# Modulation blocks moved from the first mixer to three later places in a two-block transformer kernel

## The chip, the cores and the metric

One core of a Trainium2 chip runs the whole program. The metric is the device time of one execution in microseconds (us). The kernel works in fp32: every product of two matrices is made of three matmuls (high x high, high x low, low x high) of operands that were split into a rounded part and a rest.

## The reference, cut to what matters

A first block has two layers (an even one with a Hyena and attention mixer, an odd one with a retention mixer, each with an MLP behind it); a second block follows and is not touched. Each layer's shifts, scales and gates come from a modulation: one product of two conditioning vectors with a 1024 x 6144 matrix.

```python
for i in range(DEPTH):
    mod_l = (c_act @ ada_w[i] + ada_b[i])[:, None, :]
    mod_c = cc_act @ ada_w[i] + ada_b[i]
    sh_a, sc_a, g_a, sh_m, sc_m, g_m = jnp.split(mod_l, N_MOD, axis=-1)
    ...
    h_l = modulate(rms_norm(x, norm_mix_g[i]), sh_a, sc_a)
    ...  # mixer: even or retention, gives y_l
    x = x + g_a * y_l
    x = x + g_m * sq_relu_mlp(modulate(rms_norm(x, norm_mlp_g[i]), sh_m, sc_m), mlp_w1[i], mlp_w2[i])
```

Of the second layer's modulation, the shift and scale `sh_a`, `sc_a` are wanted by the norm ahead of the retention, the gate `g_a` by the retention's out-projection, `sh_m`, `sc_m` by the norm ahead of the second MLP, and `g_m` by the end of that MLP.

## The kernel before, in words

Activations lie with features on the 128 partitions and 512 latent plus 256 context tokens along the free axis. The program (`program`, L307) goes in order through the first layer's mixer (`mixer0`), the first MLP, the retention (`retention`, four heads, two directions each), the second MLP, the second block and its expert stage.

**Modulation** (`ada`, L451). A layer's modulation has 12 blocks of 512 outputs: blocks 0 to 3 are `sh_a`, `sc_a`; 4 and 5 `g_a`; 6 to 9 `sh_m`, `sc_m`; 10 and 11 `g_m`. A block reads four chunks of 128 x 1024 fp32 (512 KB); for each chunk TensorE runs four narrow matmuls (L486; the profile counts two passes of each, so eight rows a chunk). Then ScalarE copies the sum out of PSUM (L459), two small matmuls turn it (L464, four passes), and VectorE adds the bias (L468); for blocks 3 and 9 it also makes `1 + scale` (L477).

**The weight stream** (`Stream`, L117). Every weight of the program goes through one stream, in the order in which TensorE asks for it (a first build of the program records that order). SP issues each load (L148) into one of five raw slots of 512 KB (four, and a fifth from the end of the first mixer on). A normal chunk is then split: ScalarE casts it (L155) and VectorE takes the difference (L157) into one of three pairs of split buffers, after which its raw slot is free. A modulation chunk is not split (`uncut`, L122): it keeps its raw slot until TensorE has used it (`done`, L201). So loads can run ahead of TensorE by five raw chunks and three split ones, and nothing is loaded out of order.

**The first mixer** (L703). Three generators share the stretch, drawn by a clock of given costs (`until`, L839): the in-projection with the Hyena behind it (`hy`), the attention (`attn0`), and `more` (L820), which runs the first layer's blocks 4 to 11 and then all 12 blocks of the second layer.

**Norms and tails.** A norm (`norm_mod`, L515) sums squares (L538, L541), adds over the partitions with a matmul of ones (L566), takes root and reciprocal (L502, L503), and scales, shifts and splits the eight tiles one after the other (L526, L527, L287, L288). Norms are traced as tails that run in between the next matmuls (`later`, `tick`, `settle`). The retention's last direction (L1109) ends with a norm of its own for each half of the tokens: squares (L1161, L1163), products (L1166), a matmul of ones (L1168), root and reciprocal, products (L1173), sums and splits (L1253, L287, L288); then its out-projection follows, half by half, and the second MLP, whose first group of four tiles also goes half by half (L972).

**Order on the engines.** The framework's planner runs a simulated timeline and fixes the order of the instructions on each engine, with the program's order as priority; each engine then executes its queue in that order and waits where something is late. Slots and buffers are given out by hand as the program is traced.

Of the kernel before, what the change touches and what calls it, by code (L numbers as in the profile page):

```python
# [208 lines left out]
def drain(*gens):  # L209

    gens = [list(g) if isinstance(g, tuple) else [g, 1.0] for g in gens]
    clock = [0.0] * len(gens)
    live = list(range(len(gens)))
    while live:
        i = min(live, key=lambda j: clock[j])
        try:
            clock[i] += next(gens[i][0]) / gens[i][1]
        except StopIteration:
            live.remove(i)


class K:
# [56 lines left out]
    def mm3(self, ps, wh, wl, xh, xl, start, stop):  # L279
        mm = self.nc.tensor.matmul  # L280
        mm(ps, wh, xh, start=start, stop=False)  # L281
        mm(ps, wh, xl, start=False, stop=False)  # L282
        mm(ps, wl, xh, start=False, stop=stop)  # L283

    def split(self, hi, lo, x):

# [20 lines left out]
    def program(self):  # L307
        nc = self.nc
        a = self.a
        self.ws = ws = Stream(self, self.order)  # L310
        self.phase(*MIX0)
        self.consts()
        for i in range(4):
            ws.add("cs", [a["cs_l"][i]])
        ws.add("cs", [a["cs_c"]])
        for nb in range(12):
            ws.add("ada0", [a["ada"][0, nb, i] for i in range(2)])
        order = [16, 17, 12, 13, 14, 15] + [x for c in range(4) for x in (8 + c, 4 + c)] + [0, 1, 2, 3]
        for n in range(9):
            ws.add("evin", [a["ev_in"][n]])  # L320
        self.ev_order = order
        for m in ("cs", "ics"):
            for q in "lc":
                src = a[f"{m}_{q}"]
                for i in range(4 if q == "l" else 1):
                    ws.add(m, [src[i] if q == "l" else src])
        for n in range(4):
            ws.add("evout", [a["ev_out"][n]])
            ws.add("evout_c", [a["ev_out"][n]])
        for nb in range(12):  # L330
            ws.add("ada1", [a["ada"][1, nb, i] for i in range(2)])
        G = 4
        self.G = G
        for l in range(2):
            for g in range(FF // 128 // G):
                ws.add("w1", [a["w1"][l, g * G // 2 + i] for i in range(G // 2)])
                ws.add("w2", [a["w2"][l, g, i] for i in range(G // 2)])
            ws.add("w1_b", [a["w1"][l, i] for i in range(G // 2)])
            ws.add("w2_b", [a["w2"][l, FF // 128 // G - 1, i] for i in range(G // 2)])
        for h in range(4):  # L340
            ws.add("od", [a["od_in"][h, i] for i in range(8)])
            ws.add("odo", [a["od_out"][h, i] for i in range(2)])
        ws.add("od_c", [a["od_in"][0, 1]])
        ws.add("odo_b", [a["od_out"][3, i] for i in range(2)])
        for n in range(7):
            ws.add("in2", [a["w_in2"][n]])
            ws.add("in2_b", [a["w_in2"][n]])
        for n in range(4):
            ws.add("out2", [a["w_out2"][n]])
            ws.add("out2_b", [a["w_out2"][n]])  # L350
        for n in range(8):
            ws.add("wq", [a["w_q"][n]])
            ws.add("wq_b", [a["w_q"][n]])
        ws.add("u", [a["ud"][n] for n in range(64)])
        ws.add("v", [a["vd"][n] for n in range(64)])
        ws.pump()

        self.ada_prep()
        self.maskr, self.identr = self.R(384), self.R(128)
        self.hb = [self.RP(T) for _ in range(KT)]  # L360
        self.h = [(b.hi.ap, b.lo.ap) for b in self.hb]

        def first():
            yield from self.ada(0, range(4))
            for seg in (LAT, CTX):
                for k in range(KT):
                    self.stat(k, seg)
                yield from self.norm_mod(0, 0, seg, self.h)

        self.ws.rest = nc.vector  # L370
        filt = self.hy_filter()
        drain(self.until((first(), 1.5), (filt, 1.0)))
        self.mark("mix0")
        drain(self.mixer0(filt))
        self.phase(*MLP)
        self.mark("mlp0")
        drain(self.mlp(0, True, lambda seg: self.norm_mod(1, 0, seg, self.h)))
        self.phase(*RET)
        self.mark("ret")
        drain(self.retention())  # L380
        self.phase(*MLP)
        self.mark("mlp1")
        drain(self.mlp(1, False, self.norm_final))

        for b in self.mod + self.sc1:
            b.free()
        self.phase(*B2)
        self.mark("blk2")
        drain(self.block2())
        self.phase(*PEER)  # L390
        self.mark("peer")
        drain(self.peer())
# [310 lines left out]
    def mixer0(self, filt):  # L703
        nc = self.nc
# [3 lines left out]
        qkv = self.F(6 * T)  # L708
# [4 lines left out]
        vt = self.F(6 * 128)  # L713
# [85 lines left out]
        hyx0 = self.F(4 * T)  # L799
        hyz = self.F(4 * T)  # L800
# [18 lines left out]

        def more():  # L820
            yield from self.ada(0, range(4, 12))
            yield from self.ada(1)

        yield from self.both((hy(), 1.0), (self.attn0(range(6), yah, yal), 1.2), (more(), 0.7))
        self.ws.rest = nc.vector
        self.ws.free.append(self.F(1024, top=True))
        for b in (qkv, vt, hyx0, hyz, self.maskr, self.identr, self.c32, self.kinds):
            b.free()
        yt = [t for b in (yy[0], ya) for t in self.tiles(b, T)]
        self.load_x()  # L830
# [90 lines left out]
    def mlp(self, l, ctx, then):  # L921

        nc = self.nc
# [7 lines left out]
        parts = [LAT, CTX] if ctx else HALF  # L931
# [38 lines left out]
        def w1(g):  # L970
            a = acts[g % 2]
            if g == 0:  # L972

                banks = []
                for key, (c0, c1) in zip(("w1", "w1_b"), parts):
                    for i in range(G):
                        w = self.ws.get(key)
                        ps = self.bank() if ctx or c0 == 0 else banks[i]
                        o = 0 if ctx else c0
                        gemm(w, h, 0, ps.ap[:, o : o + c1 - c0], (c0, c1))  # L980
                        self.ws.done()
                        if ctx:
                            later(up, a, i, [(ps, (c0, c1))])
                        elif c0 == 0:
                            banks.append(ps)
                        else:
                            later(up, a, i, [(ps, LAT)])
                        self.tick()
                        yield 0.01 * (c1 - c0)
                    self.settle()  # L990
                self.ws.rest = nc.vector
                return
            for i in range(G):
                w = self.ws.get("w1")
                res = [(self.bank(), seg) for seg in segs]
                for ps, seg in res:
                    gemm(w, h, 0, ps.ap[:, : seg[1] - seg[0]], seg)
                self.ws.done()
                later(up, a, i, res)
                yield 0.01 * W  # L1000
# [42 lines left out]
    def retention(self):  # L1043
        nc = self.nc
# [61 lines left out]
                a.free()  # L1106
                b.free()

        def direction(d, qk, v, tab, g, after, done, parts, add):  # L1109

            q, k = qk
            qh, ql = q.hi.v(2, S), q.lo.v(2, S)
# [22 lines left out]
            for n, (t, i0, m, m0) in enumerate(js):  # L1135
                ps = self.bank()
# [19 lines left out]
            for c0, c1 in parts:  # L1156
                m = c1 - c0
                acc = self.F(m)
                for c in range(4):
                    sq = self.F(m)  # L1160
                    nc.scalar.activation(sq.ap if c else acc.ap, o[c].ap[:, c0:c1], AF.Square)  # L1161
                    if c:
                        nc.vector.tensor_add(acc.ap, acc.ap, sq.ap)  # L1163
                    sq.free()
                for c in range(4):
                    nc.vector.tensor_mul(g[:, c, c0:c1], o[c].ap[:, c0:c1], g[:, c, c0:c1])  # L1166
                ps = self.bank()
                nc.tensor.matmul(ps.ap[:, :m], self.ones.ap, acc.ap, start=True, stop=True)  # L1168
                acc.free()
                r = self.rstd(ps.ap[:, :m], 512, m, self.eps6.ap[:, 0:1])  # L1170
                ps.free()
                for c in range(4):
                    nc.vector.tensor_mul(g[:, c, c0:c1], g[:, c, c0:c1], r.ap)  # L1173
                    if add:
                        add(c, c0, c1)
                r.free()
# [4 lines left out]
        for hd in range(4):  # L1181
# [27 lines left out]
            v = self.RP(6 * 512)  # L1209
# [15 lines left out]
            for d in range(2):  # L1225
                g = self.F(4 * S)
# [24 lines left out]
                def add(c, c0, c1):  # L1251
# [2 lines left out]
                    self.split(y.hi.v(4, S)[:, c, c0:c1], y.lo.v(4, S)[:, c, c0:c1], a)  # L1254

                yield from direction(d, (q, k), v, tabs[d], gv, after, done, HALF if d == 1 and hd == 3 else [LAT],
                                     add if d else None)
            for g in gs:
                g.free()
            prev = y  # L1260
# [1276 lines left out]
```

## Time and profile before

| | |
|---|---|
| median of 3 runs | 3834.04 us (3833.3 to 3835.98) |
| profiled execution | 3846.21 us |
| its span, first to last instruction | 3844.5 us |
| TensorE matmuls busy | 3598.5 us, 94% of the span |
| TensorE weight loads busy | 3168.7 us, 82% |
| VectorE busy | 2461.9 us, 64% |
| ScalarE busy | 1455.4 us, 38% |
| GpSimd busy | 711.4 us, 19% |
| mean granted clock of TensorE | 0.971 |

The profiled execution is a single one and slower than the runs without a profile; all durations below are its own. Busy shares are averages over stages with different limits, so the stages are read one by one. In the profile PE is TensorE's matmuls, PEld its weight loads, DVE VectorE, ACT ScalarE, POOL GpSimd, SP the engine that issues the stream's loads. A value in brackets behind a row is the idle time of the engine just ahead of it and what ended it.

### The profile page before, as it was taken

The numbers are of one execution on the slowest core, as the hardware profiler recorded it, in microseconds if no ns is written. First come the engines' busy times: TensorE is split into PE (matmuls) and PEld (weight loads), VectorE is DVE, ScalarE is ACT, GpSimd is POOL, SyncE is SP. The second block draws the span as 40 slices with busy tenths as digits, with TensorE's granted clock in tenths as the row PEclk, the third lists the DMA queues.
The fourth block names the chain that finished last, engine by engine and source line by source line (L and its number), as shares of the span: only waits on it lengthen the run. The fifth ranks groups of instructions, "written<-read, shape, count | busy, mean of one in ns | idle before, by whom it ended". The sixth has DMA issues, their size and how long they took to land. (4 is left out here: it accounts for less than half of the span.)

```text
span 3844.5 us, 51080 instructions
## 1 busy us (share of the span) xinstructions
PE 3598.5 (94%) x20063; PEld 3168.7 (82%) x20063; DVE 2461.9 (64%) x4157; ACT 1455.4 (38%) x2351; POOL 711.4 (19%) x511
## 2 busy tenths in 40 slices
PE   7999899999999999998999898888889999999997
PEld 4766588888888888887888867878789999889997
DVE  6543675343466555657544657898988777777754
ACT  5323444222244333335323546425633333332332
POOL 1111100000000000000000110665534444444200
PEclk9999999999999999998999998999999999999998
DMA  5355432212122212122322312324788888888732
GB/s 204 118 197 187 151 127 85 65 62 65 62 95 89 73 63 86 58 75 72 115 95 97 129 60 95 102 85 143 211 309 313 305 304 308 291 302 298 269 126 72
DMA packets 199597, 573.38 MB, mean 149 GB/s; under 512 B 17051, under 2 KB 67227, under 8 KB 199356
## 3 DMA queue, kind: packets, MB, share of 16 engines
q1 hardware_dynamic: 100224, 362.33, 28.7%
q0 software_dynamic: 42416, 156.57, 11.4%
q10 hardware_dynamic: 56716, 51.22, 4.0%
q8 instruction: 157, 2.57, 0.3%
q14 instruction: 84, 0.69, 0.0%
HBM read 539.64 MB, written 30.41 MB: 148 GB/s over the span
## 5 line engine op out<-in xcount | busy, mean ns | idle before, releaser
L155 ACT CAST ra<-fa 128x1024 fp32r<-128x1024 f32 x591 | 620.1, 1051 | 1591.6 <-PE P L282 655.0
L157 DVE TENSOR_TENSOR ra<-fa,ra 128x1024 fp32r<-128x1024 f32 x543 | 663.0, 1223 | 491.2 <-ACT ra L155 484.2
L282 PE MATMUL P<-ra 128*128 128x512 f32 (+1 forms) x1952 | 694.5, 357 | 2.9 <-DVE ra L288 2.7
L283 PE MATMUL P<-ra 128*128 128x512 f32 (+1 forms) x1872 | 675.3, 363 | 2.4 <-DVE ra L157 2.4
L281 PE MATMUL P<-ra 128*128 128x512 f32 (+1 forms) x1824 | 651.0, 364 | 21.1 <-ACT ra L287 17.4
L283 PE MATMUL bank<-ra 128*128 128x384 f32 (+2 forms) x1648 | 564.4, 343 | 63.1 <-DVE ra L157 41.8
L281 PE MATMUL bank<-ra 128*128 128x384 f32 (+2 forms) x1648 | 561.7, 342 | 13.0 <-ACT ra L287 11.4
L282 PE MATMUL bank<-ra 128*128 128x384 f32 (+2 forms) x1648 | 560.0, 340 | 8.3 <-DVE ra L288 8.3
L281 PE MATMUL P<-mR,ra 128*128 128x512 f32 (+1 forms) x1344 | 464.7, 349 | 12.8 <-ACT mR L287 8.6
L283 PE MATMUL P<-mR,ra 128*128 128x512 f32 (+1 forms) x1344 | 459.2, 343 | 0.3 <-DVE ra L157 0.3
L282 PE MATMUL P<-mR,ra 128*128 128x512 f32 (+1 forms) x1216 | 424.3, 350 | 1.0 <-DVE mR L288 1.0
L282 PEld LDWEIGHTS P<-ra 128*128 128x128 f32 x1952 | 375.4, 192 | 56.1 <-DVE ra L288 3.7
L281 PEld LDWEIGHTS P<-ra 128*128 128x128 f32 x1824 | 346.7, 192 | 78.7 <-ACT ra L287 19.5
L283 PEld LDWEIGHTS P<-ra 128*128 128x128 f32 x1872 | 357.9, 191 | 57.7 <-DVE ra L157 3.7
L283 PEld LDWEIGHTS bank<-ra 128*128 128x128 f32 x1648 | 317.7, 193 | 79.9 <-DVE ra L157 53.2
L281 PEld LDWEIGHTS bank<-ra 128*128 128x128 f32 x1648 | 317.8, 193 | 17.8 <-ACT ra L287 12.0
L282 PEld LDWEIGHTS bank<-ra 128*128 128x128 f32 x1648 | 317.9, 193 | 12.5 <-DVE ra L288 9.3
L876 DVE SCALAR_TENSOR_TENSOR fa<-P,fa 128x512 f32<-128x512 f32 (+1 forms) x256 | 164.1, 641 | 221.8 <-PE P L283 221.4
L281 PEld LDWEIGHTS P<-mR,ra 128*128 128x128 f32 x1344 | 257.5, 193 | 52.7 <-ACT mR L287 10.0
L283 PEld LDWEIGHTS P<-mR,ra 128*128 128x128 f32 x1344 | 256.7, 192 | 31.1 <-DVE ra L157 1.1
L282 PEld LDWEIGHTS P<-mR,ra 128*128 128x128 f32 x1216 | 232.0, 191 | 32.5 <-issue 2.2
L1968 DVE SCALAR_TENSOR_TENSOR fa<-fa 128x1024 f32<-128x1024 f32 x128 | 164.0, 1281 | 87.4 <-DMA fa<-in_vv,fa 86.9
(418 smaller groups left out, 5395.2 us busy)
## 6 DMA issues: line engine op xcount, KB each, us to landing
fa<-in_w SPq DMA_DIRECT2D x144, 512.0 KB, 3.7
fa<-in_ud SPq DMA_DIRECT2D x128, 512.0 KB, 4.8
fa<-in_vd SPq DMA_DIRECT2D x128, 512.0 KB, 5.7
fa<-in_ada SPq DMA_DIRECT2D x96, 512.0 KB, 4.9
fa<-in_od_in SPq DMA_DIRECT2D x66, 512.0 KB, 3.7
gd<-fa ACTq DMA_DIRECT2D x24, 1024.0 KB, 5.3
trio<-gd ACTq DMA_DIRECT2D x48, 512.0 KB, 9.0
fa<-in_w_q SPq DMA_DIRECT2D x22, 512.0 KB, 3.8
```

What stands on the lines that cost most here:

```text
L155: self.k.nc.scalar.copy(hi.ap, c[1].ap)
L157: eng.tensor_tensor(lo.ap, c[1].ap, hi.ap.bitcast(F32), op=OP.subtract)
L281: mm(ps, wh, xh, start=start, stop=False)
L282: mm(ps, wh, xl, start=False, stop=False)
L283: mm(ps, wl, xh, start=False, stop=stop)
L876: self.nc.vector.scalar_tensor_tensor(x, ps, g[:, n, kind : kind + 1], x, op0=OP.mult, op1=OP.add)
L1968: nc.vector.scalar_tensor_tensor(acc0.ap, r, act0.ap[:, n - 128 : n - 127], acc0.ap, op0=OP.mult, op1=OP.add)
```

## The change

Blocks 4 to 11 of the second layer's modulation leave the first mixer: `more` now ends after block 3. Blocks 4 and 5 are traced between the first MLP and the retention. Blocks 6 to 9 are traced in the last direction of the last head, behind the first half's matmul of ones, with an edge that keeps their matmuls behind it on TensorE. Block 10 is traced ahead of the second MLP's first matmul, block 11 between the two halves of its first group, behind the last matmul of the first half. The two small operands of the modulation (`c32`, `kinds`) stay allocated until the second MLP is done.

```diff
@@ mm3
-        mm(ps, wl, xh, start=False, stop=stop)
+        i = mm(ps, wl, xh, start=False, stop=stop)
+        self.last = getattr(i, "ins", i)
@@ program
         self.mark("ret")
+
+        drain(self.ada(1, range(4, 6)))
         drain(self.retention())
...
-        for b in self.mod + self.sc1:
+        for b in self.mod + self.sc1 + [self.c32, self.kinds]:
             b.free()
@@ mixer0
         def more():
             yield from self.ada(0, range(4, 12))
-            yield from self.ada(1)
+            yield from self.ada(1, range(4))
...
-        for b in (qkv, vt, hyx0, hyz, self.maskr, self.identr, self.c32, self.kinds):
+        for b in (qkv, vt, hyx0, hyz, self.maskr, self.identr):
             b.free()
@@ mlp, w1
             if g == 0:
 
+                fills = [self.ada(1, range(i, i + 1)) for i in (10, 11)] if l else []
+                for _ in fills.pop(0) if fills else ():
+                    pass
                 banks = []
                 for key, (c0, c1) in zip(("w1", "w1_b"), parts):
...
                         yield 0.01 * (c1 - c0)
+                    with self.tc.issue_after(self.last):
+                        for _ in fills.pop(0) if fills else ():
+                            pass
                     self.settle()
@@ retention, direction
-        def direction(d, qk, v, tab, g, after, done, parts, add):
+        def direction(d, qk, v, tab, g, after, done, parts, add, fill):
...
                 ps = self.bank()
-                nc.tensor.matmul(ps.ap[:, :m], self.ones.ap, acc.ap, start=True, stop=True)
+                i = nc.tensor.matmul(ps.ap[:, :m], self.ones.ap, acc.ap, start=True, stop=True)
                 acc.free()
+                with self.tc.issue_after(getattr(i, "ins", i)):
+                    for _ in fill:
+                        pass
                 r = self.rstd(ps.ap[:, :m], 512, m, self.eps6.ap[:, 0:1])
...
                 yield from direction(d, (q, k), v, tabs[d], gv, after, done, HALF if d == 1 and hd == 3 else [LAT],
-                                     add if d else None)
+                                     add if d else None, self.ada(1, range(6, 10)) if d == 1 and hd == 3 else ())
```

## Rows read from the trace of the kernel before

**Rows 1.** Stretches: start:end, length, busy us and instructions by engine, TensorE clock, DMA share, GB/s.

```profile
core 0: us, PE busy (x) PEld busy (x) DVE busy (x) ACT busy (x) POOL busy (x), PEclk, DMA share, GB/s
313.00:413.00 100.00, 96.45 (x760) 66.19 (x758) 46.62 (x105) 34.24 (x86) 10.54 (x6) 1.00 0.60 198
413.00:470.00 57.00, 49.38 (x258) 32.70 (x260) 35.65 (x95) 27.79 (x82) 14.38 (x15) 0.85 0.35 116
...
1113.00:1129.00 16.00, 11.99 (x42) 9.74 (x43) 14.64 (x27) 14.50 (x25) 0.53 (x1) 0.79 0.33 115
...
1769.00:1776.00 7.00, 0.88 (x4) 0.88 (x5) 6.74 (x17) 2.68 (x8) 0.00 (x0) 0.50 0.00 0
1776.00:1802.00 26.00, 25.42 (x192) 25.03 (x191) 23.57 (x45) 11.99 (x20) 0.00 (x0) 0.91 0.38 125
...
304.00:308.00 4.00, 3.32 (x14) 2.03 (x15) 0.64 (x2) 0.00 (x0) 2.14 (x1) 0.50 0.78 290
...
170.00:178.00 8.00, 6.36 (x47) 3.25 (x45) 5.13 (x16) 4.84 (x18) 3.60 (x2) 1.00 0.95 342
```

**Rows 2.** TensorE's timeline at the three later places: start, length, line, tile, count.

```profile
1117.01 0.79 PE L281 MATMUL P<-ra 128*128 128x512 f32 x1 [4.46 <-ACT ra L287]
...
1767.08 1.11 PE L1168 MATMUL P<-mF,fa 128*128 128x256 f32 x2 [1.90 <-DVE mF L1163]
1775.12 1.44 PE L281 MATMUL P<-mR,ra 128*128 128x256 f32 x5 [6.92 <-ACT mR L287]
...
1804.03 0.70 PE L566 MATMUL P<-fa 128*128 128x256 f32 x2 [2.61 <-DVE fa L541]
1809.11 0.80 PE L281 MATMUL P<-ra 128*128 128x256 f32 x2 [4.38 <-ACT ra L287]
```

**Rows 3.** SP's issues (first start, first to last issue) and landings, 1680 to 1800 us.

```profile
1688.81 60.21 SPq L148 DMA_DIRECT2D fa<-in_od_out  x8
...
DMA to landing us min/median/max: 3.5/3.7/4.6
```

**Rows 4.** TensorE's timeline in the first mixer, one chunk and one finish.

```profile
351.33 0.64 PE L486 MATMUL P<-fa 128*32 128x256 f32 x8
351.90 0.44 PE L2275 MATMUL P<-fa,mF 128*128 128x128 f32 x2
...
358.20 0.50 PE L464 MATMUL P<-fa 128*128 128x4 f32 x4
358.56 0.47 PE L281 MATMUL P<-mR,ra 128*128 128x512 f32 x1
```

**Rows 5.** Groups by line on TensorE, 313 to 413 us: busy us, mean ns, idle before.

```profile
L486 PE MATMUL P<-fa 128*32 128x256 f32 x272 | 20.3, 388 | 2.4 <-DMA fa<-in_ada 2.4
...
L464 PE MATMUL P<-fa 128*128 128x4 f32 x32 | 4.1, 235 | 0.0
```

**Rows 6.** DMA: 40 slices of 296 to 312 us; sum of 160 to 420 us.

```profile
GB/s 0 41 0 133 348 256 338 174 195 297 266 307 256 266 215 215 205 246 277 358 369 420 410 399 307 195 41 184 266 307 338 195 41 20 20 0 0 0 0 0
...
DMA packets 13755, 50.27 MB, mean 193 GB/s; under 512 B 1533, under 2 KB 1533, under 8 KB 13734
```

**Rows 7.** The page's costliest groups: the two halves of a weight split.

```profile
L155 ACT CAST ra<-fa 128x1024 fp32r<-128x1024 f32 x591 | 620.1, 1051 | 1591.6 <-PE P L282 655.0
L157 DVE TENSOR_TENSOR ra<-fa,ra 128x1024 fp32r<-128x1024 f32 x543 | 663.0, 1223 | 491.2 <-ACT ra L155 484.2
```

**Rows 8.** VectorE: groups of 1776 to 1802 us, and one row of its timeline.

```profile
L288 DVE TENSOR_TENSOR mR<-fa,mR 128x256 fp32r<-128x256 f32 x7 | 2.7, 415 | 0.0
...
L503 DVE RECIPROCAL fa<-fa 128x256 f32<-128x256 f32 x1 | 1.8, 1752 | 1.0 <-ACT fa L502 1.0
L1253 DVE TENSOR_TENSOR fa<-fa,mF 128x256 f32<-128x256 f32 x4 | 1.5, 414 | 0.0
L1173 DVE TENSOR_TENSOR mF<-mF,fa 128x256 f32<-128x256 f32 x4 | 1.4, 420 | 0.0
...
1803.56 0.42 DVE L541 TENSOR_TENSOR fa<-fa 128x256 f32<-128x256 f32 x1
```

## The prediction

> **What bounds the kernel now.** TensorE is busy for 94% of the span, so the question at each place the change touches is whether TensorE works or waits there, and on what. I read the stretches by engine first [rows 1]. Between 313 and 413 us, the part of the first mixer in which the blocks that leave are computed, TensorE is busy for 96.45 of 100 us at full clock, VectorE for 46.62: TensorE's own queue sets the pace, and what is taken out of it there should come off the time. Then the waits in TensorE's timeline at the three places that receive blocks [rows 2]: it stands for 4.46 us before the retention's first projection (it stops at 1112.55), for 1.90 and 6.92 us around the last direction's norm, and for 2.61 and 4.38 us before the second MLP. All end on ScalarE or VectorE, that is on a norm's chain. These 20.3 us are what the change can fill for nothing. But a block needs four chunks of 512 KB from HBM as well, and only five raw slots exist. How far loads run ahead is seen in SP's issues: eight chunks (five raw, three already split) are issued before TensorE reaches the first one, and a lone load lands after 3.7 us [rows 3]. Modulation chunks are never split, so each holds its raw slot until TensorE has multiplied it. That is the fact on which the forecast turns.
>
> **The first mixer: less 20 us.** Eight blocks leave, 32 chunks and 8 finishing steps. From start to next start a chunk of eight matmul passes takes 0.57 us (351.33 to 351.90) and a finish 0.36 (358.20 to 358.56) [rows 4]; the rows of the whole stretch hold 272 such passes (34 chunks) in 20.3 us and 32 finishing passes (eight finishes) in 4.1 us, with 2.4 us of idle time, all of it waits for the modulation's loads [rows 5]. So 32 x 0.55 = 17.6, 8 x 0.44 = 3.5 (0.36 to 0.51 by these rows) and 2.4: 23.5 us at most. The attention that runs beside it loses a filler. Where it has none, from 413 to 470 us, TensorE is busy for only 49.38 of 57 us [rows 1]; the same 13% of the remaining 76 us would expose 10 us and leave a gain of 13.5. But from 313 to 413 the in-projection's matmuls stay as filler (they need nothing from attention), so I take 3.5 us exposed: -20, between -23.5 and -13.5. The 32 loads, 32 releases of slots, 8 ScalarE copies and the small VectorE additions move along; none of them bounds this stretch. On SP's queue the in-projection's and the transform's loads come earlier, which helps nobody who waits; POOL's queue carries none of the moved steps.
>
> **The price of a load in a row.** At the new places chunks come one behind the other through five slots. In the mixer's dense stretches the DMA moved 342 GB/s (170 to 178 us) [rows 1], 1.53 us per chunk; its best slices reach 420 GB/s, 1.25 us [rows 6]; the mean from 160 to 420 us, where requests are not always waiting, is 193 GB/s, 2.7 us [rows 6]. Five slots at 1.5 us are 7.5 us, longer than the 3.7 us of a lone load and TensorE's 0.57, so the queue stays filled and I take 1.5 us, the value of a filled queue; 1.25 and 2.7 stay as ends.
>
> **Blocks 4 and 5, ahead of the retention: +5 us.** When TensorE stops at 1112.55, five modulation chunks lie ready; nothing of the retention's weights does, since they stand behind chunks 6 to 8 in SP's queue. Chunk 6 is issued when the first slot is free, about 1113.2, and lands at 1116.9; two more chunks and the first weight chunk at 1.5 us each: 1121.4. ScalarE's cast takes 1.05 us [rows 7], so the projection starts near 1122.4 in place of 1117.01: +5.4. The norm's tail then no longer slows it (the clock from 1113 to 1129 is 0.79 on the mean, VectorE busy for 14.64 of 16 us [rows 1]), so I take +5; ends +2 (nothing holds these two blocks back, so the planner may run some chunks inside the MLP's last pass, which would be the change not doing what it says) and +9 (2.7 us a chunk). The VectorE additions queue in the norm's chain for well under 1 us and nobody waits for them here.
>
> **Blocks 6 to 9, in the last direction's norm: +15 us, then 8 back.** The edge holds them behind the matmul of ones at 1767.08 to 1768.2. Five chunks are there, eleven follow and then the out-projection's first. At the lower clock (0.50 from 1769 to 1776 [rows 1]) a chunk takes twice 0.57, so the first slot is free near 1768.9 and chunk 6 lands at 1772.6; eleven loads later, at 1789.1, the first out-projection chunk is there; cast, 1790.2. It now starts at 1775.12: +15.1 (12.3 at 1.25 us, 28 at 2.7). What waits behind it: all of the out-projection, whose eight chunks are there by 1753 today [rows 3].
> Part comes back. From 1776 to 1802 VectorE is busy for 23.57 of 26 us [rows 1], and 7.4 us of that is the second half's norm (reciprocal 1.8, two products 1.4 and 1.5, splits 2.7) [rows 8]. The first half's statistics therefore end only at 1803.56 [rows 8], which is why TensorE stands from 1801.42 to 1809.11 [rows 2]. With the change the second half's norm is done inside the new wait. Against it, three weight splits of 1.22 us [rows 7] that were done early enter the pass. VectorE then needs some 21 of the pass's 25 us ahead of the MLP's first tile, and the 7.7 us wait, 1.1 us of the moved ones matmul and some 2.8 us of a first tile that runs at the lower clock would go: 11.6 at most, 0 if the planner keeps today's order. I take 10 because a split may come late, less 2.2 us for block 10, which no wait would hide any more (4 x 0.55; if the wait stays, it hides it): together +15 - 10 + 2.2 = +7, between +3 and +28.
>
> **Block 11, between the MLP's two halves: +2.5 us.** TensorE shows no wait there, so 2.2 us are paid in full; its chunks hold four of five slots, so the second half's second chunk may be 0 to 1 us late; ends +1 and +4. Keeping the two small operands allocated until after the second MLP shifts addresses and costs nothing that a row shows; +-2 us for what the planner makes of it.
>
> **Sum.** -20 + 5 + 7 + 2.5 = -5.5, say -6. The profiled execution, 3846.2 us (span 3844.5), would become 3840. It stands 12 us over the median of the runs shown, 3834.0; I take the same difference there: 3828. A measurement here can tell 0.2%, 7.7 us, from no change.
>
> The clock is an open point: from 304 to 308 us, where TensorE waited for a modulation chunk, the granted clock was 0.50 [rows 1]. The Trainium skill, "TensorE: Matmul & The Clock Gate", section "Loop structure matters more than you think", speaks against loops in which TensorE waits for a DMA between short bursts, because the bursts and what follows run at the lower clock; by that rule the out-projection and the MLP's first tile stay slow too, the 2.8 us above are not won, and the sum is about -3. The trace agrees where it shows such waits, by the 0.50 just named.
>
> **The rivals.**
> Better than that: the mixer gives back all of 23.5 us, the loads run at 1.25 us. Then 4.7 before the retention, 12.3 - 11.6 + 2.2 = 2.9 in the next place, 2.2 for block 11: -14, 3820. For it: TensorE's 96% in that stretch; against it: the 13% of idle time behind it. Chance 0.28.
> Slower: the five-slot ring does not stay filled. A slot is released by TensorE, whose queue is in order; if a block's finishing matmul waits there for its ScalarE copy, or the second half's matmul of ones for its sum, the releases behind it wait too, and a chunk costs 2.7 us. There are 14 such spacings ahead of a first weight chunk (3 and 11): +16.8, +11 in all, 3845. It decides from 1.9 us a chunk, where the whole change is worth nothing; from 2.5 us it is a measurable loss. For it: the mean of 193 GB/s; against it: 342 GB/s in stretches with the same interleaving. Chance 0.17.
> No give-back: the planner keeps the order of statistics and splits, and the 7.7 us wait stays behind the longer one, with block 10 hidden in it: -20 + 5 + 15 + 2.5 = +2.5, 3836.5. Chance 0.15.
> The forecast itself, 3821 to 3836, has 0.40.
>
> **How the numbers follow.** Of the forecast's 0.40 about a third lies beyond 0.2% (0.14), of the better case 0.27: faster 0.41. Slower: 0.15 of its case and 0.02 of the one without give-back, 0.17. The rest, 0.42, is within 0.2%. The range leaves out the far end of each outer case: 3814 to 3845.
>
> **What would show it.** In the changed profile: from 313 us on no modulation pass, and mixer work ending some 20 us earlier; before the retention a TensorE wait that ends on a modulation load, and a first projection 9 to 10 us after the MLP's last matmul; after the last direction's matmul of ones 16 chunks of modulation spread over some 20 us, each waiting for its load, 1.25 to 1.7 us apart; a wait before the second MLP that is short or gone. I am wrong if those chunks come far closer together or further apart, if TensorE idles in the shortened mixer by more than 5 us, or if the wait before the second MLP stays.

## The result, and the profile after

3862.49 us (median; 3855.47 to 3865.37) against 3834.04: ratio 1.0061, 95% interval 1.005 to 1.0073. By the ratio the changed kernel is some 23 us slower (the two medians differ by 28 us; later medians of the kernel before are 3836.6 to 3837.3). Predicted were 3828 us and a range of 3814 to 3845. The profiled execution took 3862.49 us, its span 3860.8. A second profile of the kernel before (below) has a span of 3839.6.

To compare stages, six points are marked in each profile. t1 is the end of the first MLP's matmuls, t2 the first matmul of the retention, t3 the last direction's product of ones (the first half's), t4 the first matmul of its out-projection, t5 the first of the second MLP, and t6 SP's issue of that MLP's 37th weight load. The third row is a run in which blocks 4 to 11 are left out altogether (us):

| kernel | to t1 | t1-t2 | t2-t3 | t3-t4 | t4-t5 | t5-t6 | t6-end |
|---|---|---|---|---|---|---|---|
| before, second profile | 1107.9 | 4.5 | 650.1 | 8.0 | 34.0 | 147.8 | 1887.2 |
| changed | 1081.6 | 12.3 | 658.3 | 22.8 | 44.7 | 157.0 | 1884.1 |
| without blocks 4 to 11 | 1076.8 | 4.5 | 654.1 | 8.0 | 33.9 | 147.3 | 1881.7 |

From the third row to the second, t1 to t6 grows by 7.8 + 4.2 + 14.7 + 10.7 + 9.7 = 47 us. That is what the moved blocks cost where they went; the forecast had 14.5. The code behind t6 is the same in all kernels, and yet t6 to the end lies between 1878.7 and 1886.8 us in the twelve profiles of other kernels, against 1887.2 and 1887.6 in the two of the kernel before. Whether the change has a part in that is not known.

The page's busy times of the changed kernel show none of this; TensorE stays at 94%:

```profile
PE 3614.7 (94%) x20063; PEld 3181.2 (82%) x20063; DVE 2460.3 (64%) x4157; ACT 1456.2 (38%) x2351; POOL 712.7 (18%) x511
```

**The mixer.** Stretches of the second profile of before, from 280 us to the out-projection's first load (columns as in [rows 1]), then of the changed kernel:

```profile
280.00:467.00 187.00, 172.47 (x1208) 118.83 (x1206) 91.82 (x220) 71.14 (x188) 29.45 (x23) 0.95 0.50 167
```

```profile
280.00:443.00 163.00, 149.92 (x931) 109.89 (x930) 89.47 (x217) 69.32 (x185) 28.95 (x23) 0.96 0.27 88
```

TensorE's busy time falls by 22.6 us and its idle time by 1.4: the attention does not miss its filler. Another 2.3 us come off by t1.

**The three places.** TensorE's timeline of the changed kernel, answering to [rows 2]:

```profile
1081.54 2.37 PE L489 MATMUL P<-fa 128*32 128x256 f32 x40
...
1086.03 0.64 PE L489 MATMUL P<-fa 128*32 128x256 f32 x8 [1.41 <-DMA fa<-in_ada]
1088.64 0.94 PE L489 MATMUL P<-fa 128*32 128x256 f32 x8 [1.97 <-DMA fa<-in_ada]
...
1093.88 0.79 PE L281 MATMUL P<-ra 128*128 128x512 f32 x1 [1.41 <-ACT ra L155]
...
1752.86 2.37 PE L489 MATMUL P<-fa 128*32 128x256 f32 x40
...
1758.16 1.08 PE L489 MATMUL P<-fa 128*32 128x256 f32 x8 [2.27 <-DMA fa<-in_ada]
...
1770.56 2.96 PE L489 MATMUL P<-fa 128*32 128x256 f32 x24
1774.07 1.01 PE L467 MATMUL P<-fa,mF 128*128 128x4 f32 x4 [0.55 <-ACT mF L462]
1775.01 0.58 PE L281 MATMUL P<-mR,ra 128*128 128x256 f32 x1
...
1789.77 0.58 PE L281 MATMUL P<-mR,ra 128*128 128x256 f32 x1 [3.67 <-ACT ra L155]
...
1813.95 3.64 PE L489 MATMUL P<-fa 128*32 128x256 f32 x32 [3.55 <-ACT fa L505]
```

Five chunks run at once (x40), then TensorE waits for loads, as forecast: for all three that are left ahead of the retention, and for six of the eleven in the last direction. What the forecast does not have is the wait in the middle of the out-projection, for a weight's cast (L155). ScalarE's casts there, and SP's issues of the loads that they wait for:

```profile
1773.91 1.05 ACT L155 CAST ra<-fa 128x1024 fp32r<-128x1024 f32 x1
...
1781.09 1.04 ACT L155 CAST ra<-fa 128x1024 fp32r<-128x1024 f32 x1 [3.17 <-DMA fa<-in_od_out]
...
1788.67 1.05 ACT L155 CAST ra<-fa 128x1024 fp32r<-128x1024 f32 x1 [1.60 <-DMA fa<-in_od_out]
...
1795.29 1.05 ACT L155 CAST ra<-fa 128x1024 fp32r<-128x1024 f32 x1 [1.85 <-DMA fa<-in_od_out]
```

```profile
1768.39 0.33 SPq L148 DMA_DIRECT2D fa<-in_od_out  x1
...
1776.25 0.33 SPq L148 DMA_DIRECT2D fa<-in_od_out  x1
...
1783.42 0.33 SPq L148 DMA_DIRECT2D fa<-in_od_out  x1
...
1791.00 0.33 SPq L148 DMA_DIRECT2D fa<-in_od_out  x1
```

From the second on, each of these loads is issued only when the cast before it and its difference (some 2.3 us) are done, and it lands 4 to 5 us later: 7 us a chunk, where TensorE needs 3. The first weights behind a run of modulation chunks take turns in one raw slot of the five. The code says why. While the program is traced, `pump` lets the cutting pointer (the place in the stream up to which chunks are split) step over modulation chunks that are not used yet. So the first weight behind them is cut as soon as it has a slot. Its slot goes to the next weight, that one is cut too, and so on, while the other four slots still hold modulation. Those four go to the fifth weight and the three behind it, and SP issues these as soon as the slots are free, before the second: five loads by 1773.6 us (SP's loads of that line from 1753 to 1775 us),

```profile
L148 SPq DMA_DIRECT2D fa<-in_od_out x5: 327/328/328, 1768.4 to 1773.6; - x5
```

then one every 7 us. That nothing is loaded out of order, as said above of the kernel before, does not hold here.

The same shows once more ahead of the second MLP. The last wait in TensorE's rows (3.55 us, for the root L505 of that MLP's norm) ends late because the root stands in ScalarE's queue behind a weight's cast, and that cast waits for its load:

```profile
1812.48 1.04 ACT L155 CAST ra<-fa 128x1024 fp32r<-128x1024 f32 x1 [2.89 <-DMA fa<-in_w]
1813.43 0.47 ACT L505 ACTIVATE fa<-P,fa 128x256 f32<-128x256 f32 x1
```

### The profile page after: what moved, and what is told of

The parts are those of the page before. It is cut to its first block, busy times and chain, and to the rows that moved or that the text cites. A ratio compares the mean times of both kernels' runs of the same rounds, so it can differ in the third digit from the quotient of the medians.

```text
span 3860.8 us, 51067 instructions
## 1 busy us (share of the span) xinstructions
PE 3614.7 (94%) x20063; PEld 3181.2 (82%) x20063; DVE 2460.3 (64%) x4157; ACT 1456.2 (38%) x2351; POOL 712.7 (18%) x511
## 5 line engine op out<-in xcount | busy, mean ns | idle before, releaser
L155 ACT CAST ra<-fa 128x1024 fp32r<-128x1024 f32 x591 | 620.5, 1051 | 1601.8 <-PE P L282 655.5
L281 PE MATMUL P<-ra 128*128 128x512 f32 (+1 forms) x1824 | 657.7, 365 | 19.5 <-ACT ra L288 12.3
```

The source lines that it names most:

```text
L155: self.k.nc.scalar.copy(hi.ap, c[1].ap)
```

## The experiments

**A second profile of before**, and **blocks 4 to 11 left out** (`ada(1, range(4, 6))`, `range(6, 10)` and the fills 10, 11 removed; their part of the modulation set to 0.5).

> The kernel before once more, for a second profile of it: the first one stood 9 to 12 us over the median of its runs. If that excess lies in the first mixer, the loads of the out-projection there come 5 to 10 us earlier than in the first profile, and the mixer's gain of 31 us by the two profiles is really 21 to 26 us; if it lies elsewhere, they come within 2 us.

3841.27 us, span 3839.6. It reaches t1 4.6 us earlier than the first, and keeps that distance to the end: so far the excess was in the mixer, and the mixer's gain is 26 us rather than 31.

> Changed kernel with blocks 4 to 11 of the second layer's modulation left out altogether (their part of the modulation is a constant), so that only the first mixer's part of the change is left. Theory A (the mixer gained 31 us, as the loads behind it show): 28 to 33 us faster than the kernel before, about 3804 us, so that the moved blocks cost 55 to 60 us where they went. Theory B (the mixer gained the 20 us of the prediction, and the rest of the 31 us was clock or drift of one profile): 18 to 23 us faster, about 3814 us.

3808.96 us, ratio 0.9937 (0.9921 to 0.9952), which is 24 us: between the two theories. But t2 to t3 is 4.0 us longer than before, and it is 653 to 659 us in every kernel of this document that keeps `c32` and `kinds` and has no blocks inside the retention. In the run without blocks this is 1 us in each head. There a Silu comes ahead of a head's root and its table load on ScalarE, and the root starts 3.7 us after its product of ones, where it was 1.1 us. So the mixer gives some 28 us, if t6 to the end is taken as equal. The figures "to t1" of the eight kernels without blocks 4 to 11 in the mixer lie between 1076.8 and 1082.5, a scatter of 6 us.

**The pointer held.** In `pump`, with `hold` set behind the first mixer:

```diff
             elif self.split < self.loaded and self.order[self.split][0] in self.uncut:
+                if self.hold and self.split > len(self.asked):
+                    return
                 self.split += 1
```

> Changed kernel with one rule added to the weight stream from the first MLP on: its cutting pointer may not pass a modulation chunk that has not been asked for yet, so the weight chunks behind a run of modulation chunks stay in their own raw slots instead of being cut one by one into the slot of the first. Theory A (the weights behind the modulation chunks all go through one raw slot, about 7 us each: load, cast, difference, next load): the first four out-projection loads land about 1.4 us apart right behind the last modulation chunk instead of 7 us apart, the out-projection's waits (3.7 us and the late casts) go, and the same at block 5 and at block 10; 10 to 18 us faster than the changed kernel, about 3845 us. Theory B (the order of the second half's squares behind the modulation copies is what costs the time, the slots do not matter): within 4 us of the changed kernel, 3858 to 3866 us.

3851.42 us, ratio 1.0034 (1.002 to 1.0048): 10 us faster than the changed kernel, theory A at its lower end. t2 to t3 falls from 658.3 to 652.7, t4 to t5 from 44.7 to 37.7. The casts now have their data (same rows as above):

```profile
1768.11 1.05 ACT L155 CAST ra<-fa 128x1024 fp32r<-128x1024 f32 x1
...
1769.65 1.04 ACT L155 CAST ra<-fa 128x1024 fp32r<-128x1024 f32 x1
...
1771.13 1.04 ACT L155 CAST ra<-fa 128x1024 fp32r<-128x1024 f32 x1
...
1775.35 1.05 ACT L155 CAST ra<-fa 128x1024 fp32r<-128x1024 f32 x1 [2.23 <-PE P L284]
```

t5 to t6 did not get better (159.0): that part of the expectation failed. And the out-projection still waits, now for the second half's splits, so theory B was not wrong either:

```profile
1787.49 0.97 PE L283 MATMUL P<-mR,ra 128*128 128x256 f32 x6 [2.74 <-ACT mR L290]
1790.25 0.58 PE L284 MATMUL P<-mR,ra 128*128 128x256 f32 x1 [1.79 <-DVE mR L291]
```

**The second half's squares first**, alone and with the pointer held: squares, gate products and both products of ones stand ahead of `for _ in fill`.

> Changed kernel with only the order in the last retention direction changed: the squares, sums and gate products of both halves, and the product of ones of both, stand ahead of blocks 6 to 9 instead of the first half's alone. Theory A (one raw slot): the second half's norm is ready early, but the out-projection's chunks still come 7 us apart, so only the waits for the second half go: 0 to 5 us faster than the changed kernel, about 3860 us. Theory B (order of the squares): the second half's wait that the earlier kernel had lies under the modulation blocks, 8 to 12 us faster, about 3852 us.

> Both edits together: the cutting pointer held, and the squares of both halves ahead of blocks 6 to 9. Theory A: the two waits of the second half and the 7 us steps go together, 18 to 25 us faster than the changed kernel, 3838 to 3845 us, within 0.3% of the kernel before. Theory B: no more than the order alone gives, about 3852 us.

3863.91 us (1.0079, 1.0061 to 1.0096) and 3848.6 us (1.0032, 1.0021 to 1.0043): the order gains nothing, neither against the changed kernel nor against the held pointer, and none of the four expected times came. The stages show that the edit did two things. t4 to t5 falls by 3.6 us alone, and with the pointer held from 44.7 to 34.2, which is nearly all that was lost there. But the edge now hangs on the second half's product of ones, so the blocks start 7 us later: t3 to t4 is 33.5 and 31.7. Hence the next one, in which they hang on the first half's:

```diff
+                sums.append((ps, getattr(i, "ins", i)))
+            with self.tc.issue_after(sums[0][1]):
+                for _ in fill:
+                    pass
+            for (c0, c1), (ps, _) in zip(parts, sums):
```

> The cutting pointer held, the squares of both halves ahead of blocks 6 to 9 in the program, but the blocks released by the first half's product of ones, not by the second's, so that they start 7 us earlier than in the run with both edits and the second half's norm lies inside the blocks. Theory A+B (one slot and order of the squares add up between the out-projection's start and the MLP's, 5.6 and 3.4 us of the 10.5 lost there): from the first product of ones to the MLP's first matmul about 58 us, against 65.9 with both edits and 67.4 in the changed kernel; 6 to 8 us faster than with both edits, about 3841 us, within 0.2% of the kernel before. Theory D (the modulation's loads set the start of the out-projection and what follows is bound by VectorE whatever the order): the 7 us come back as a wait before the MLP, 3847 to 3852 us.

3841.78 us, ratio 1.0014 (1.0004 to 1.0023); t3 to t5 59.3 us. Theories A and B add up: the two orders are 18 of the 47 us. Against the held pointer alone, t3 to t5 falls only from 61.7 to 59.3; t5 to t6 falls from 159.0 to 151.2, which the expectation did not have. Theory D is half right as well, since a wait of 3.92 us ahead of the MLP stays:

```profile
1797.85 0.60 PE L572 MATMUL P<-fa 128*128 128x256 f32 x2
...
1799.20 1.93 PE L492 MATMUL P<-fa 128*32 128x256 f32 x32
1801.62 0.61 PE L470 MATMUL P<-fa,mF 128*128 128x4 f32 x4 [0.49 <-ACT mF L465]
1806.15 0.79 PE L283 MATMUL P<-ra 128*128 128x256 f32 x2 [3.92 <-ACT ra L290]
```

It is not VectorE's load, though. The first half's last sum of squares ends at 1795.39, and the product of ones (L572) stands 2.5 us later in TensorE's order. From it to the MLP's first tile the norm's chain takes 8.3 us, against 5.1 in [rows 2], and block 10 covers the first half of that. In the second half the tile's split (L290) stands on ScalarE behind a weight's cast that waits for its load, which makes 2.8 us from the end of L533 to the split:

```profile
1801.78 1.08 ACT L533 ACTIVATE fa<-fa 128x256 f32<-128x256 f32 x2
1804.75 1.04 ACT L155 CAST ra<-fa 128x1024 fp32r<-128x1024 f32 x1 [1.89 <-DMA fa<-in_w]
1805.70 0.40 ACT L290 CAST ra<-fa 128x256 fp32r<-128x256 f32 x1
```

So a weight that comes late behind block 10 holds up the MLP even with the pointer held.

**One place at a time**, by the changed kernel's own stream; the other blocks are back in the mixer.

> The changed kernel's blocks 10 and 11 alone, by its own stream; blocks 4 to 9 are back in the first mixer. The mixer gains a quarter of 24 to 30 us, 6 to 7.5 us. Theory A (one slot for the weights behind each block, 9.7 us lost in the MLP's first group in the changed kernel): 8 to 11 us paid, 3838 to 3841 us, not faster than the kernel before. By the forecast's own terms (block 10 hidden in the wait that stays here, block 11 at 2.5 us): 3 us paid, 3832 to 3834 us.

3851.1 us, ratio 1.0033 (1.002 to 1.0047): 13 us slower, beyond both expectations. t4 to t5 is 33.8, so block 10 costs nothing in the wait; t5 to t6 is 161.1, 13.8 us more than without blocks. The mixer does not show its expected gain of 6 to 7.5 us: this profile reaches t1 at 1107.5, 0.4 us earlier than before, within the scatter of 6. SP's issues behind t5, the casts, and TensorE's longest wait:

```profile
1802.06 0.33 SPq L148 DMA_DIRECT2D fa<-in_w  x1
...
1807.84 0.33 SPq L148 DMA_DIRECT2D fa<-in_w  x1
...
1817.57 0.33 SPq L148 DMA_DIRECT2D fa<-in_w  x1
...
1826.13 0.33 SPq L148 DMA_DIRECT2D fa<-in_w  x1
```

```profile
1805.51 1.04 ACT L155 CAST ra<-fa 128x1024 fp32r<-128x1024 f32 x1 [1.56 <-DMA fa<-in_w]
...
1815.24 1.04 ACT L155 CAST ra<-fa 128x1024 fp32r<-128x1024 f32 x1 [1.35 <-DMA fa<-in_w]
...
1823.80 1.05 ACT L155 CAST ra<-fa 128x1024 fp32r<-128x1024 f32 x1 [1.79 <-PE P L282]
...
1829.79 1.04 ACT L155 CAST ra<-fa 128x1024 fp32r<-128x1024 f32 x1 [0.80 <-DMA fa<-in_w]
...
1839.37 1.04 ACT L155 CAST ra<-fa 128x1024 fp32r<-128x1024 f32 x1 [1.28 <-DMA fa<-in_w]
```

```profile
1840.46 0.58 PE L281 MATMUL P<-ra 128*128 128x256 f32 x1 [4.39 <-ACT ra L155]
```

One weight load is in flight at a time, issued 6 to 10 us apart, until block 11 gives its four slots back.

> The changed kernel's blocks 6 to 9 alone, by its own stream; blocks 4, 5, 10 and 11 are back in the first mixer. The mixer gains half of 24 to 30 us, 12 to 15 us. Theory A+B (15 us for the loads, then 7 us more in the out-projection through the one slot and the late second half): 22 us paid, about 3845 us, 0.2% slower than the kernel before. By the forecast's own terms (15 us paid, 10 given back): 5 us paid, about 3828 us.

3848.29 us, ratio 1.0033 (1.0022 to 1.0043). t3 to t4 is 25.5, t4 to t5 39.6: 23 us paid, as theory A+B has it (17.5 for the loads, 5.7 behind them).

**No run longer than the ring, or no run at all.** `next(extra, None)` behind each `ws.done()` of the retention's `project`, with `extra = self.ada(1, range(4, 12))`:

> Blocks 4 to 11 are computed one chunk after each weight chunk of the retention's projections, not in a run, and fill no wait. Theory A (the cost of the moved blocks is the run of modulation chunks, which empties the ring of weights): only TensorE's own time is paid, 8 x (4 x 0.57 + 0.36) = 21 us over the run without these blocks, so about 3830 us, within 0.2% of the kernel before. Theory C (any modulation chunk behind the first mixer holds back weights through its raw slot, one by one too): waits for weights after most of the 32 chunks, 1 us or more each, 3860 us or later.

3842.88 us, ratio 1.0018 (1.0009 to 1.0027). Theory C does not happen: TensorE idles for 7.4 us in all from t2 to t3, against 3.8 without blocks. But t2 to t3 grows by 32.6 us, not 21: 20.4 us are the passes and finishes from start to start, 3.6 more waits, and 8.6 are in the other matmuls; a clock of 0.94 instead of 1.00 in one stretch of 30 us is 2 of these, and what the rest is stays open. A block costs 3.9 us here (ratio against that without blocks, over eight) and about 3.5 in the mixer.

> Only as many chunks as the ring already holds go into a wait: block 4 ahead of the retention, block 6 behind the first product of ones of the last direction; blocks 5 and 7 to 11 one chunk after each weight chunk of the retention's projections; pointer held, squares of both halves first. Theory A: the two runs of four chunks lie under the waits of 4.5 and 7 us for no more than 2 us each, six blocks cost 2.64 us each, 16 us: about 24 us gained in the mixer against 18 to 20, 3831 to 3834 us, the best of the versions here by a little. Theory D (a run of four chunks still pushes the weights behind it past the wait): 3 to 5 us more at each of the two places, 3838 to 3844 us.

> Only blocks 4 and 6 leave the first mixer, each a run of four chunks, as many as the ring already holds, into the wait ahead of the retention and into that behind the first product of ones; pointer held, squares of both halves first; the other ten blocks stay in the mixer. Theory A (a run no longer than the ring lies under the wait): two blocks at 3.0 us each off the mixer, 0 to 3 us paid back, 3830 to 3834 us, at or just under the kernel before by less than 0.2%. Theory D (even four chunks push the weights behind them past the wait, 3 to 5 us at each place): 3837 to 3841 us.

> As the run with blocks 4 and 6, and block 10 as well leaves the mixer for the wait ahead of the second MLP. Theory A: its 3.2 us lie under the wait of 2.6 and 4.4 us there, 3 us more are gained, 3828 to 3832 us, up to 0.2% faster than the kernel before. Theory D: its four chunks take the slots of the MLP's first weights, whose waits give the 3 us back, 3833 to 3837 us.

3836.49 us (0.9998, 0.9985 to 1.001), 3839.02 (1.0003, 0.9994 to 1.0012) and 3838.36 (0.9997, 0.9986 to 1.0009): each as fast as the kernel before, none faster. With two blocks moved, t1 to t2 still grows by 2.3 us and t3 to t4 by 1.9; with block 10 as well, t4 to t5 grows by 4.4, and there too the MLP's first tile stands behind a cast that waits 2.09 us for its load. The small runs cost what they save, nearer to theory D than to A. No version that computes all blocks beats the kernel before.

## Why the prediction was wrong

The forecast was 6 us faster, the measurement 23 us slower. Of the 29 us between them the moved blocks are 33 (47 instead of 14.5) and the retention's 4 us with the two operands kept; the mixer gave 8 more than forecast.

- **The step that failed: what comes behind a run.** At each place the prediction followed the loads up to "the first weight chunk" or "the first out-projection chunk" and stopped there; the weights behind it got no term. They came 7 us apart through one slot. Shown by holding the pointer: 5.7 us in the retention's first projections, 7.0 in the out-projection. The same fault is in the rows of the MLP's first group when blocks 10 and 11 move alone; holding the pointer did not mend that place, where eight modulation chunks stand among the first eight weights.
- **"Part comes back", 10 us.** Nothing did: t4 to t5 grew by 10.7 us where -7.8 was written. The end at 0, "if the planner keeps today's order", was seen, but not an end above it. Its own sign of being wrong came: the wait before the second MLP stayed. Against the run without blocks the 10.7 are: waits +2.1 (9.1 against 7.0), block 10 4.7 instead of 2.2, the same 192 matmuls 29.8 us instead of 25.3 start to start, less 0.5 for the products of ones. The second half's norm was not done in the new wait: three of its four squares (L1170) ran only from 1775.18 us on, behind the copies of the modulation (L462) in ScalarE's queue:

```profile
1773.64 0.37 ACT L462 COPY mF<-P 128x256 f32<-128x256 f32 x1 [4.82 <-PE P L489]
1773.91 1.05 ACT L155 CAST ra<-fa 128x1024 fp32r<-128x1024 f32 x1
1775.18 0.39 ACT L1170 ACTIVATE mF<-P 128x256 f32<-128x256 f32 x1 [0.22 <-PE P L467]
```

  With both orders mended, t4 to t5 is 1 us shorter than without blocks, with block 10 in it: 3 to 4 us come back, no more.
- **The clock.** Block 10's 4.7 us and the slower 192 matmuls are one thing, the lower clock behind waits:

```profile
1775.00:1811.00 36.00, 30.86 (x197) 28.82 (x196) 27.76 (x53) 14.29 (x25) 0.00 (x0) 0.81 0.47 156
1811.00:1840.00 29.00, 22.82 (x180) 18.48 (x181) 20.06 (x40) 18.25 (x40) 0.00 (x0) 0.82 0.49 165
```

  The granted clock is 0.81 and 0.82 on the mean, so part of both stretches ran at 1.2 GHz instead of 2.4 (columns as in [rows 1]; [rows 1] have 0.91 for the out-projection). The MLP's first stage, t5 to t6, paid another 3.7 us in slower matmuls, at 0.96 against 0.98 without blocks. The prediction put the lower clock at 2.8 us. The section of the Trainium skill that it cited, "TensorE: Matmul & The Clock Gate", "Loop structure matters more than you think", has a matmul behind a long wait for a DMA run at the lower clock. The trace agrees, by the 0.81 and 0.82 behind these waits, and it cost more than the prediction allowed.
- **Block 11, +2.5.** t5 to t6 grew by 9.7: waits 3.7, slower matmuls 3.7, block 11 itself 2.3.
- **Blocks 4 and 5, +5.** The first projection came 7.8 us later (1.41, 1.97 and 1.41 us of waits in the rows above), the next ones lost 4.2: 12.
- **The loads of blocks 6 to 9, +15.1.** Right: t3 to t4 grew by 14.7, and the eleven chunks that were not there yet landed 1.43 us apart (1758.11 to 1772.40), where 1.5 was taken. Where these blocks move alone it is 17.5.
- **The mixer, -20, at most -23.5.** Too small: 26 by the profiles, 28 by the run without blocks, each with the scatter named above. No part of it was exposed. 22.6 us is TensorE's own work, where the sum has 21.1 (17.6 and 3.5); the rest is waits and the out-projection behind it.
- **The two operands, 0.** They go with 4 us in the retention. Every kernel that keeps them has also lost blocks from the mixer, and what causes the 4 us was not tried by itself.
- **The rivals.** "No give-back" was the right one in kind, at 0.15; none had the weights behind a run. The rival for a slower kernel had another cause, modulation loads 2.7 us apart, and they came at 1.43.
- **What stays open.** With both orders mended t1 to t6 still costs 29 us, twice the forecast. By stages these are 18.4 up to the out-projection (the loads of blocks 6 to 9), 8.4 ahead of the retention and 3.9 in the MLP's first stage, less 2 in the others. None of them was taken out by an experiment.

The Trainium skill, "Perfetto Trace Analysis", section "Optimization Strategy", says that a gap that repeats on the engine that should be busy can mean too little room for the next tile. The repeated gap ahead of the casts looks like that, but the room was the same five slots in the run that had no such gap; what differed was who was given the slot that came free.

## What to carry to other kernels

When something is put into an in-order stream of loads, follow the stream past it: write down the slot, issue and landing of each of the next loads, not of the first alone. A wait can be filled for nothing only with operands that are there already, and in the runs with two and three blocks moved even a run of four chunks cost 1.9 to 4.4 us at each place. A run longer than the ring turned the wait into a queue for the DMA and left an empty ring behind, and the waits it made cost their length and the clock after them. An edge that fixes where work starts can undo a better order, so read each stage's time and not the total.

## What the runs showed of the hardware

With the queue full, loads of 512 KB on one core landed 1.43 us apart (379 GB/s on the mean from 1760 to 1775 us of the changed kernel); the best slice of [rows 6], 420 GB/s, would be 1.25 us. One at a time, the same load took 3.5 to 3.8 us from issue to landing in the retention's last out-projection of the kernel before, and 4.3 and 4.8 us in the changed kernel's out-projection; why is not shown. The figures "to t1" differ by up to 6 us between profiles with the same mixer code, while the stretch from the first load of the mixer's out-projection to t1, 638.5 us, repeats to 0.1 us in all twelve kernels other than before.
